# Block products of the gate/up weights in the second half's FFN, from weight sums kept in DRAM

## The chip, the core and the metric

The kernel runs on one core of one Trainium2 chip. The metric is the time of one execution on the device in microseconds (us), from runs on the chip. A core has TensorE (PE: matmuls, with PEld its weight loads), VectorE (DVE), ScalarE (ACT), GpSimd (POOL) and SyncE (SP). Each engine works through its own instructions in the order in which they stand in the built program and waits at semaphores for the others. SP and POOL issue DMA transfers. Matmuls write to PSUM, which the kernel uses in banks of 512 columns; the other tiles lie in SBUF.

## The reference, cut to what matters

One layer: a conditioned norm, two branches (a gated linear recurrence and chunked linear attention), their merge, and a feed-forward network (FFN). There are 1024 tokens of a prompt and 32 of a sample group (8 sequences of 4), D_MODEL is 1024 and D_FF 2816, all in fp32. What is changed is the first product of the FFN:

```
h2 = _rmsnorm(x, norm2_g) * (1.0 + sc2) + sh2
f1, f2 = jnp.split(h2 @ ffn_w1, 2, axis=-1)
x = (x + gt2 * ((jax.nn.silu(f1) * f2) @ ffn_w2))
```

## The kernel before

Activations lie with features on the 128 partitions and tokens on the columns. `h2` is 8 tiles of 128 features (the k tiles). The kernel works the tokens in two halves one after the other: half A has 512 prompt tokens, half B the other 512 and the 32 sample tokens, 544 columns, in two parts of 272 (p0, p1). Names end in `a` or `b` for the half.

Every fp32 operand is split in two: hi is the operand rounded to the type fp32r (a copy on ScalarE, L141), lo the rest (a subtraction on VectorE, L142). A product takes three matmuls for each k tile and part (L365 to L367 in `gemm`): hi by hi, hi weights by lo input, lo weights by hi input. `load_raw` gets a weight tile of 128 x 1024 from DRAM through SP into one of three `raw` buffers; `split_w` writes it, hi and lo, into one of three `hl` buffers, with a raised priority.

The FFN has 22 couples, one gate tile (`f1`) and one up tile (`f2`) of 128 rows of ffn_w1 each. `pair` computes a couple: the gate product into one PSUM tile, tanh and a VectorE operation for the silu, the up product into a second PSUM tile, the multiplication with it, and the split of the result `fa` for the second FFN product. In half B a PSUM tile (pool `mm`) has two banks, and there are three of them; in half A six of one bank.

`back` sets the order at the FFN: output projection, norm2, then couples 0 to 3 (EARLY) first for part p0 and then, in reverse, for part p1 (`ffn1_first`, woven into the norm by `mix`), then couples 4 to 10 for the whole half (`ffn1`), then the first half of the second FFN product (`ffn2`). Couples 11 to 21 follow in the main program at the end of the function. A scheduler that has a model of the engines puts the instructions of each engine in order; a product may be interleaved with others there.

Of the kernel before, what the change touches and what calls it, by code (L numbers as in the profile page):

```python
# [7 lines left out]
F32 = mybir.dt.float32  # L8
F32R = mybir.dt.float32r
I32 = mybir.dt.int32  # L10
AF = mybir.ActivationFunctionType
OP = mybir.AluOpType
# [3 lines left out]
P = 128  # L16
# [11 lines left out]
LEVELS = (64, 32, 16, 8, 4, 2, 1)  # L28
EPS = 1e-6
EARLY = 4  # L30
AHEAD = 70
def starts_of(w):
    return [min(i, w - P) for i in range(0, w, P)]
# [19 lines left out]
def hybrid_layer(ctx, tc, I, O):  # L53
# [17 lines left out]
    xp = ctx.enter_context(tc.tile_pool(name="xp", bufs=8))  # L71
    tp = ctx.enter_context(tc.tile_pool(name="tp", bufs=6))
    axp = ctx.enter_context(tc.tile_pool(name="axp", bufs=2, space=PSUM))

    def S(name, dt=F32):
        return sbig.tile([P, 2 * 544], dt, tag="S", name=name)
# [216 lines left out]
    def drain(g):  # L293
        for _ in g:
            pass
# [29 lines left out]
    class Half:  # L325
# [23 lines left out]
        def psv(s, ps, part):  # L349
            return s.pv(ps) if part[2] is None else ps[:, part[2], part[3]:part[3] + part[1]]  # L350

        def gemm(s, ps, hl, nk, rhs, k0=0, first=True, last=True, part=None, hk=0, split=None):
            N = s.N
            if part is None:
                pieces = split or ([(0, HP, 0, 0)] if s.hf == 0 else s.parts)
            else:
                pieces = [part]
            for kt in range(nk):
                x = rhs[k0 + kt]
                wh = hl[:, 0, (hk + kt) * P:(hk + kt + 1) * P]  # L360
                wl = hl[:, 1, (hk + kt) * P:(hk + kt + 1) * P]
                st, en = first and kt == 0, last and kt == nk - 1
                for o, w, bank, off in pieces:
                    out = ps[:, bank, off:off + w]
                    pe.matmul(out, wh, x[:, o:o + w], start=st, stop=False)  # L365
                    pe.matmul(out, wh, x[:, N + o:N + o + w], start=False, stop=False)  # L366
                    pe.matmul(out, wl, x[:, o:o + w], start=False, stop=en)  # L367
# [777 lines left out]
        def pair(s, f, part, a):  # L1145

            n = f"{s.n}{f}{part[2]}{part[0]}"
            whole = part[2] is None
            gp = None if whole else part
            ti = (lambda t: s.sv(t)) if whole else (lambda t: t)  # L1150
            o, w = part[0], part[1]
            p1 = mm("f1ps" + n)
            fr = not whole and o == 0
            s.gemm(p1, load_kept(("f1", f), I["ffn1"][2 * f], 1024, "f1" + n, fr and f == EARLY - 1), 8, s.h2, part=gp)
            yield w * 24 / 2400.0
            tg = T("ft" + n)[:, :w]
            v1 = s.psv(p1, part)
            act.activation(ti(tg), v1, AF.Tanh, scale=0.5)
            dve.scalar_tensor_tensor(ti(tg), ti(tg), 1.0, v1, op0=OP.add, op1=OP.mult)
            p2 = mm("f2ps" + n)  # L1160
            s.gemm(p2, load_kept(("f2", f), I["ffn1"][2 * f + 1], 1024, "f2" + n, fr and f >= EARLY - 2), 8, s.h2, part=gp)
            dve.tensor_mul(ti(tg), ti(tg), s.psv(p2, part))
            hi, lo = a[:, o:o + w], a[:, s.N + o:s.N + o + w]
            act.activation(hi, tg, AF.Copy)
            dve.tensor_sub(lo, tg, hi.bitcast(F32))
            yield w * 24 / 2400.0

        def ffn1_first(s, part, n):
            for f in range(n) if part[0] == 0 else range(n - 1, -1, -1):
# [44 lines left out]
        def back(s):  # L1214
# [12 lines left out]
            next(f)  # L1227
            mix(s.norm2(p1, a1), f)
            drain(f)
            drain(s.ffn1_first(p1, EARLY))  # L1230
            drain(s.ffn1(0, EARLY))
            drain(s.ffn2(0, s.whole))

        def branches(s, before):
# [49 lines left out]
    drain(dn)  # L1284
    mm_pool(2)
    B.branches(A.finish(A.whole, acc))
    drain(B.ffn1(1))
    p0, p1 = B.parts
    a0, a1 = [ACC("30b")], [ACC("31b")]
    drain(B.ffn2(1, p0, a0))  # L1290
# [32 lines left out]
def _pack(inp):  # L1323
# [30 lines left out]
    a["proj_b"] = _tiles(f["proj_b"][0])  # L1354
    a["w_out"] = _tiles(f["w_out"][0])
    w1 = _tiles(f["ffn_w1"][0])
    a["ffn1"] = c(w1.reshape(2, NF, P, D).transpose(1, 0, 2, 3).reshape(2 * NF, P, D))
    w2 = _tiles(f["ffn_w2"][0])
    a["ffn2"] = c(w2.reshape(KD, P, 2, 11 * P).transpose(0, 2, 1, 3).reshape(2 * KD, P, 11 * P))
# [39 lines left out]
```

## Time and profile before

| | before |
|---|---|
| time, median of 3 runs | 2015.49 us (2014.96 to 2020.08) |
| the profiled execution: time | 2014.85 us |
| the profiled execution: span of the trace | 2013.1 us |
| half A, couples 4 to 10 | from 661 to 736 us of the span |
| half B, early couples, second part | 1627.4 to 1651.5 us |
| half B, couples 4 to 10 | 1651.5 to 1735 us |
| half B, couples 11 to 21 | 1803 to 1935 us |

The span runs from the first to the last instruction in the trace; the time holds what lies around it too. The page gives busy time by engine, in all and in slices, the waits and the chain of work that ended last; the tables of windows give the same for a stretch of time. A row of a group has its line, engine and operation, what it writes and reads, how often it occurs, its busy time in us with the mean in ns, and the idle time just before it with what ended that. In a timeline the first two columns are start and duration in us. The trace gives a matmul of 272 columns a duration of 0.29 us while the next one starts 0.125 us after it: the pace is seen in the distance of starts.

### The profile page before, as it was taken

To read this page: it belongs to the slowest core of one execution; us is meant where nothing else is said; L and a number is where in the kernel's file an instruction comes from. 1 tells how busy PE (TensorE), PEld (TensorE's weight loads), DVE (VectorE), ACT (ScalarE), POOL (GpSimd) and SP (SyncE) were. 2 spreads that over 40 slices of the span, in tenths; PEclk is the share of its full clock that TensorE was granted. 3 is DMA by queue.
4 is the path that set the end of the run, shared out by engine and by line. 5 is a ranking of instruction groups with operands and counts; after the bars stand their busy time and mean duration, and the time that the engine had idled before them with its cause. 6 is when DMAs were issued, how large, how long until landed. Compare 5 with 4: busy or idle time off the path is not lost. (4 is left out here: it accounts for less than half of the span.)

```text
span 2013.1 us, 31675 instructions
## 1 busy us (share of the span) xinstructions
PE 1982.9 (99%) x13210; PEld 1782.5 (89%) x13210; DVE 1086.7 (54%) x1828; ACT 806.0 (40%) x1165; POOL 51.3 (3%) x122
## 2 busy tenths in 40 slices
PE   8999999999999999999999999999999999999997
PEld 5887777777899888888899999999999999999997
DVE  5648485544457433346473697863434763333356
ACT  3545475533245322233352465653323442222232
POOL 0000010000000000000000001110000000000000
PEclk9999999999999999999999999999999999999998
DMA  8325233334354323332422313223223442232243
GB/s 311 105 95 178 61 93 109 111 116 162 98 169 146 115 77 112 99 135 81 148 72 90 117 53 115 101 91 105 85 89 117 160 134 92 73 105 89 84 122 123
DMA packets 74639, 228.50 MB, mean 114 GB/s; under 512 B 8704, under 2 KB 16640, under 8 KB 74496
## 3 DMA queue, kind: packets, MB, share of 16 engines
q1 hardware_dynamic: 71536, 217.47, 33.6%
q0 software_dynamic: 2416, 8.44, 1.1%
q8 instruction: 104, 1.70, 0.4%
q10 hardware_dynamic: 544, 0.56, 0.1%
q14 instruction: 39, 0.32, 0.1%
HBM read 217.21 MB, written 9.23 MB: 112 GB/s over the span
## 5 line engine op out<-in xcount | busy, mean ns | idle before, releaser
L367 PE MATMUL f3psb<-fab,f3b_hl 128*128 128x272 f32 x352 | 101.4, 288 | 0.0
L365 PE MATMUL f3psb<-fab,f3b_hl 128*128 128x272 f32 x352 | 101.4, 288 | 0.0
L366 PE MATMUL f3psb<-fab,f3b_hl 128*128 128x272 f32 x352 | 100.9, 287 | 0.0
L141 ACT ACTIVATE f3b_hl<-f3b_raw 128x768 fp32r<-128x768 f32 (+1 forms) x45 | 35.7, 792 | 88.6 <-PE f3psb L367 57.2
L365 PE MATMUL f3psa<-faa,f3a_hl 128*128 128x512 f32 x176 | 68.7, 390 | 0.0
L367 PE MATMUL f3psa<-faa,f3a_hl 128*128 128x512 f32 x176 | 68.5, 389 | 0.0
L366 PE MATMUL f3psa<-faa,f3a_hl 128*128 128x512 f32 x176 | 68.5, 389 | 0.0
L365 PEld LDWEIGHTS f3psb<-fab,f3b_hl 128*128 128x128 f32 x352 | 66.4, 189 | 0.0
L367 PEld LDWEIGHTS f3psb<-fab,f3b_hl 128*128 128x128 f32 x352 | 66.2, 188 | 0.0
L366 PEld LDWEIGHTS f3psb<-fab,f3b_hl 128*128 128x128 f32 x352 | 66.1, 188 | 0.0
L142 DVE TENSOR_TENSOR f3b_hl<-f3b_raw,f3b_hl 128x768 fp32r<-128x768 f32 (+1 forms) x45 | 40.1, 892 | 35.5 <-ACT f3b_hl L141 35.2
L141 ACT ACTIVATE f3a_hl<-f3a_raw 128x768 fp32r<-128x768 f32 (+1 forms) x32 | 25.4, 793 | 84.2 <-PE f3psa L367 47.8
L142 DVE TENSOR_TENSOR f3a_hl<-f3a_raw,f3a_hl 128x768 fp32r<-128x768 f32 (+1 forms) x32 | 28.5, 890 | 39.0 <-ACT f3a_hl L141 38.3
L365 PE MATMUL uxpsb<-h1b,uxpsb_hl 128*128 128x256 f32 (+1 forms) x160 | 47.1, 294 | 0.1
L366 PE MATMUL uxpsb<-h1b,uxpsb_hl 128*128 128x256 f32 (+1 forms) x160 | 46.4, 290 | 0.0
L365 PE MATMUL ugpsb<-h1b,ugpsb_hl 128*128 128x272 f32 x160 | 46.3, 289 | 0.0
L367 PE MATMUL ugpsb<-h1b,ugpsb_hl 128*128 128x272 f32 x160 | 46.1, 288 | 0.0
L367 PE MATMUL uxpsb<-h1b,uxpsb_hl 128*128 128x256 f32 (+1 forms) x160 | 45.9, 287 | 0.0
L366 PE MATMUL ugpsb<-h1b,ugpsb_hl 128*128 128x272 f32 x160 | 45.8, 286 | 0.0
L367 PEld LDWEIGHTS f3psa<-faa,f3a_hl 128*128 128x128 f32 x176 | 33.0, 188 | 7.1 <-DVE f3a_hl L142 0.2
L366 PEld LDWEIGHTS f3psa<-faa,f3a_hl 128*128 128x128 f32 x176 | 33.1, 188 | 6.9
L365 PEld LDWEIGHTS f3psa<-faa,f3a_hl 128*128 128x128 f32 x176 | 33.0, 188 | 6.7
(1495 smaller groups left out, 7057.2 us busy)
## 6 DMA issues: line engine op xcount, KB each, us to landing
ada<-in_ada_w SPq DMA_DIRECT2D x48, 512.0 KB, 5.4
f3b_raw<-in_ffn SPq DMA_DIRECT2D x23, 384.0 KB, 3.1
f3b_raw<-in_ffn SPq DMA_DIRECT2D x22, 320.0 KB, 2.9
woa_raw<-in_w_out SPq DMA_DIRECT2D x13, 512.0 KB, 3.5
wob_raw<-in_w_out SPq DMA_DIRECT2D x13, 512.0 KB, 3.4
f3a_raw<-in_ffn SPq DMA_DIRECT2D x16, 384.0 KB, 3.1
uxpsa_raw<-in_w_in SPq DMA_DIRECT2D x10, 512.0 KB, 3.7
ugpsa_raw<-in_w_in SPq DMA_DIRECT2D x10, 512.0 KB, 3.6
```

The source lines that it names most:

```text
L141: act.activation(hl[:, 0, :n], raw[:, :n], AF.Copy)
L142: dve.tensor_sub(hl[:, 1, :n], raw[:, :n], hl[:, 0, :n].bitcast(F32))
L365: pe.matmul(out, wh, x[:, o:o + w], start=st, stop=False)
L366: pe.matmul(out, wh, x[:, N + o:N + o + w], start=False, stop=False)
L367: pe.matmul(out, wl, x[:, o:o + w], start=False, stop=en)
```

## The change

The couples 4 to 21 of half B take a scheme of Strassen's kind. The k tiles are taken as even (0, 2, 4, 6) and odd (1, 3, 5, 7), the output rows as gate and up, the columns as two parts of 272. Of these 2 x 2 x 2 blocks, eight products of 4 k tiles each become seven, of sums of blocks. The seven are called 11, t1, t2, 22, t3, 21 and t4 after the inputs that they use.

- Weight sums: when half A works a couple (4 to 21), `weight_sums` makes four sums of blocks of the raw gate and up weights on VectorE (512 columns each) and POOL sends them to DRAM (`wsum`, two transfers of 512 KB). The raw tiles of both weights are held until then.
- Input sums: `block_sums` makes the sums of blocks of `h2` and splits them, on VectorE and ScalarE. It is mixed into the p1 pass of the early couples. The result t3 is written over the columns of p0 in the even tiles.
- Products: `ffn1_fast` reads 7 blocks of 512 columns a couple, as pairs in a raw tile, four of them from `wsum`. 11, t2, t3 and t4 add up in one bank of PSUM tile x (`f1ps`), t1 and 22 in the other; 21 goes to tile y (`f2ps`). Between them ScalarE copies the running values out (`snap`, into `va` and `vb`), and VectorE adds the rest.
- `pair` and the packing of ffn_w1 use the k tiles in the order KORD, evens first, in both halves.

In half B the couples after the change have no `pair`; in half A and in the early couples they have.

On TensorE, at the start of couple 7 of half B (`f1psb7` is its tile x): before, the gate product runs through its k tiles, three rows for each.

```order
L365 MATMUL f1psb7None0_15133<-h2b00_14027,f1b7None0_hl_15136 128x272 [waits DVE_49,Activation_49]
L366 MATMUL f1psb7None0_15133<-h2b00_14027,f1b7None0_hl_15136 128x272
L367 MATMUL f1psb7None0_15133<-h2b00_14027,f1b7None0_hl_15136 128x272 [waits DVE_49]
L365 MATMUL f1psb7None0_15133<-h2b00_14027,f1b7None0_hl_15136 128x272
L366 MATMUL f1psb7None0_15133<-h2b00_14027,f1b7None0_hl_15136 128x272
```

After, the end of couple 6's t4 (input `t42`), the last row of couple 7's 11 (input `h2b06`) and the start of its t1 (inputs `t120`, `t121`):

```order
L1241 MATMUL f1psb6_15270<-t42_14772,fwb420_hl_15378 128x272
L1242 MATMUL f1psb6_15270<-t42_14772,fwb420_hl_15378 128x272
L1242 MATMUL f1psb7_15397<-h2b06_14299,fwb420_hl_15378 128x272
L1240 MATMUL f1psb7_15397<-t120_14738,fwb422_hl_15418 128x272 [waits Activation_49]
L1241 MATMUL f1psb7_15397<-t120_14738,fwb422_hl_15418 128x272
L1242 MATMUL f1psb7_15397<-t120_14738,fwb422_hl_15418 128x272
L1240 MATMUL f1psb7_15397<-t121_14755,fwb422_hl_15418 128x272
```

The first row of t1 waits for ScalarE right behind the last row of 11; t4 of the couple before has been put in front of that last row.

On ScalarE, the same couple after the change; `vab7` and `vbb7` are the copies out of tile x, `fwb..._hl` the splits of weights, `ftb` tanh, `fab` the hi part of a result:

```order
L1246 ACTIVATE vab7_15399<-f1psb7_15397 128x272 [waits PE_49]
L145 ACTIVATE fwb426_hl_15482<-fwb426_15479 128x1024 [waits DMAHW7_49,DMAHW6_49,Activation_49]
L1274 ACTIVATE fab6_15269<-ftb6_15274 128x544 [waits DVE_49]
L1246 ACTIVATE vbb7_15400<-f1psb7_15397 128x272 [waits PE_49]
L1246 ACTIVATE vab7_15399<-f1psb7_15397 128x272 [waits PE_49]
L145 ACTIVATE fwb428_hl_15526<-fwb428_15523 128x1024 [waits DMAHW1_49,DMAHW0_49,Activation_49]
L1246 ACTIVATE vbb7_15400<-f1psb7_15397 128x272 [waits PE_49]
```

Four copies a couple stand among the splits, each with a wait for TensorE; before, ScalarE had one operation a couple that reads each gate product, and no copy.

On VectorE, in the p1 pass of half B's early couples, from the end of couple 3's p0 part (`ftb300`) on. Before:

```order
L1162 TENSOR_TENSOR ftb300_14502<-ftb300_14502,f2psb300_14505 128x272 [waits DVE_49,PE_49]
L445 SCALAR_TENSOR_TENSOR h2b07_14140<-xn2b2727_14494,mod_98,h2b07_14140 128x272 [waits Activation_49]
L1165 TENSOR_TENSOR fab3_14455<-ftb300_14502,fab3_14455 128x272 [waits Activation_49]
L142 TENSOR_TENSOR f1b21272_hl_14597<-f1b21272_raw_14595,f1b21272_hl_14597 128x1024 [waits DMAHW7_49,Activation_49]
L1159 SCALAR_TENSOR_TENSOR ftb31272_14563<-ftb31272_14563,f1psb31272_14538 128x272 [waits Activation_49]
```

After:

```order
L1171 TENSOR_TENSOR ftb300_14666<-ftb300_14666,f2psb300_14669 128x272 [waits DVE_49,PE_49]
L1196 TENSOR_TENSOR d00_14727<-h2b00_14191 128x544
L449 SCALAR_TENSOR_TENSOR h2b07_14304<-xn2b2727_14658,mod_118,h2b07_14304 128x272 [waits Activation_49]
L1174 TENSOR_TENSOR fab3_14619<-ftb300_14666,fab3_14619 128x272 [waits Activation_49]
L1196 TENSOR_TENSOR d10_14728<-h2b01_14196 128x544
L1197 TENSOR_TENSOR ta0_14729<-d00_14727 128x272 [waits DVE_49]
L1199 TENSOR_TENSOR tb0_14730<-d10_14728,d00_14727 128x272 [waits DVE_49]
L1198 TENSOR_TENSOR ta0_14729<-d10_14728,ta0_14729 128x272 [waits DVE_49]
L146 TENSOR_TENSOR f1b21272_hl_14831<-f1b21272_raw_14829,f1b21272_hl_14831 128x1024 [waits DMAHW7_49,Activation_49]
L1200 TENSOR_TENSOR tb0_14730<-d10_14728,ta0_14729 128x272 [waits DVE_49]
```

The operation that reads `f1psb31272` (couple 3's gate product for p1) and so frees that PSUM tile came one split later; now 23 operations of the block sums stand ahead of it, of which the piece shows the first.

The diff, without some of its context:

```diff
 EARLY = 4
+KORD = (0, 2, 4, 6, 1, 3, 5, 7)
+QW = 272
...
     xp = ctx.enter_context(tc.tile_pool(name="xp", bufs=8))
     tp = ctx.enter_context(tc.tile_pool(name="tp", bufs=6))
     axp = ctx.enter_context(tc.tile_pool(name="axp", bufs=2, space=PSUM))
+    drp = ctx.enter_context(tc.tile_pool(name="drp", bufs=1, space=bass.MemoryType.DRAM))
+    wsum = {f: drp.tile([P, 2048], F32, name=f"wsum{f}") for f in range(EARLY, NF)}
     def S(name, dt=F32):
         return sbig.tile([P, 2 * 544], dt, tag="S", name=name)
...
         def psv(s, ps, part):
             return s.pv(ps) if part[2] is None else ps[:, part[2], part[3]:part[3] + part[1]]
-        def gemm(s, ps, hl, nk, rhs, k0=0, first=True, last=True, part=None, hk=0, split=None):
+        def gemm(s, ps, hl, nk, rhs, k0=0, first=True, last=True, part=None, hk=0, split=None, order=None):
             N = s.N
             if part is None:
                 pieces = split or ([(0, HP, 0, 0)] if s.hf == 0 else s.parts)
             else:
                 pieces = [part]
             for kt in range(nk):
-                x = rhs[k0 + kt]
+                x = rhs[order[kt] if order else k0 + kt]
                 wh = hl[:, 0, (hk + kt) * P:(hk + kt + 1) * P]
                 wl = hl[:, 1, (hk + kt) * P:(hk + kt + 1) * P]
                 st, en = first and kt == 0, last and kt == nk - 1
...
             o, w = part[0], part[1]
             p1 = mm("f1ps" + n)
             fr = not whole and o == 0
-            s.gemm(p1, load_kept(("f1", f), I["ffn1"][2 * f], 1024, "f1" + n, fr and f == EARLY - 1), 8, s.h2, part=gp)
+            r1 = r2 = None
+            if whole:
+                r1, r2 = load_raw(I["ffn1"][2 * f], 1024, "f1" + n), load_raw(I["ffn1"][2 * f + 1], 1024, "f2" + n)
+            s.gemm(p1, split_w(r1, 1024, "f1" + n) if whole else load_kept(("f1", f), I["ffn1"][2 * f], 1024, "f1" + n, fr and f == EARLY - 1), 8, s.h2, part=gp, order=KORD)
             yield w * 24 / 2400.0
             tg = T("ft" + n)[:, :w]
             v1 = s.psv(p1, part)
             act.activation(ti(tg), v1, AF.Tanh, scale=0.5)
             dve.scalar_tensor_tensor(ti(tg), ti(tg), 1.0, v1, op0=OP.add, op1=OP.mult)
             p2 = mm("f2ps" + n)
-            s.gemm(p2, load_kept(("f2", f), I["ffn1"][2 * f + 1], 1024, "f2" + n, fr and f >= EARLY - 2), 8, s.h2, part=gp)
+            s.gemm(p2, split_w(r2, 1024, "f2" + n) if whole else load_kept(("f2", f), I["ffn1"][2 * f + 1], 1024, "f2" + n, fr and f >= EARLY - 2), 8, s.h2, part=gp, order=KORD)
+            if whole:
+                s.weight_sums(f, r1, r2)
             dve.tensor_mul(ti(tg), ti(tg), s.psv(p2, part))
             hi, lo = a[:, o:o + w], a[:, s.N + o:s.N + o + w]
             act.activation(hi, tg, AF.Copy)
             dve.tensor_sub(lo, tg, hi.bitcast(F32))
             yield w * 24 / 2400.0
+        def weight_sums(s, f, r1, r2):
+            u, v = S(f"wu{f}"), S(f"wv{f}")
+            dve.tensor_add(u[:, 0:512], r2[:, 0:512], r2[:, 512:1024])
+            dve.tensor_sub(u[:, 512:1024], u[:, 0:512], r1[:, 0:512])
+            dve.tensor_sub(v[:, 512:1024], r1[:, 0:512], r2[:, 0:512])
+            dve.tensor_sub(v[:, 0:512], r1[:, 512:1024], u[:, 512:1024])
+            pool.dma_start(wsum[f][:, 0:1024], u[:, :1024])
+            pool.dma_start(wsum[f][:, 1024:2048], v[:, :1024])
+        def block_sums(s):
+            N, W = s.N, QW
+            s.bs = {k: [] for k in ("11", "21", "22", "t1", "t2", "t3", "t4")}
+            t4 = None
+            for i in range(4):
+                h0, h1 = s.h2[2 * i], s.h2[2 * i + 1]
+                d0, d1, ta, tb = T(f"d0{i}"), T(f"d1{i}"), T(f"ta{i}"), T(f"tb{i}")
+                for d, h in (d0, h0), (d1, h1):
+                    dve.tensor_add(d, h[:, :N].bitcast(F32), h[:, N:2 * N].bitcast(F32))
+                dve.tensor_sub(ta[:, :W], d0[:, :W], d0[:, W:])
+                dve.tensor_sub(ta[:, W:], d1[:, :W], ta[:, :W])
+                dve.tensor_sub(tb[:, :W], d1[:, :W], d0[:, :W])
+                dve.tensor_sub(tb[:, W:], d1[:, W:], ta[:, W:])
+                if i % 2 == 0:
+                    t4 = S(f"t4{i}", F32R)
+                t12 = S(f"t12{i}", F32R)
+                o4 = i % 2 * W
+                for t, o, src in (t12, 0, ta), (t4, o4, tb[:, W:]), (h0, 0, tb[:, :W]):
+                    w = 2 * W if src is ta else W
+                    act.activation(t[:, o:o + w], src, AF.Copy)
+                    dve.tensor_sub(t[:, N + o:N + o + w], src, t[:, o:o + w].bitcast(F32))
+                for k, t, o in (("11", h0, W), ("21", h1, W), ("22", h1, 0), ("t1", t12, 0), ("t2", t12, W),
+                                ("t3", h0, 0), ("t4", t4, o4)):
+                    s.bs[k].append((t, o))
+                yield 1.0
+        def ffn1_fast(s, fs):
+            N, W = s.N, QW
+            units = []
+            for f in fs:
+                w1, w2, sm = I["ffn1"][2 * f], I["ffn1"][2 * f + 1], wsum[f]
+                units += [w1[:, 0:512], sm[:, 0:512], sm[:, 512:1024], sm[:, 1024:1536], sm[:, 1536:2048], w1[:, 512:1024],
+                          w2[:, 512:1024]]
+            now = [0, None]
+            def weights():
+                u = now[0]
+                now[0] += 1
+                if u % 2 == 0:
+                    raw = wp.tile([P, 1024], F32, tag="raw", name=f"fw{s.n}{fs[0]}{u}")
+                    two = units[u:u + 2]
+                    for j, src in enumerate(two):
+                        sp.dma_start(raw[:, j * 512:(j + 1) * 512], src)
+                    now[1] = split_w(raw, 512 * len(two), f"fw{s.n}{fs[0]}{u}")
+                return now[1], u % 2 * 512
+            def product(out, key, first):
+                hl, c = weights()
+                for i, (x, o) in enumerate(s.bs[key]):
+                    wh, wl = hl[:, 0, c + i * P:c + (i + 1) * P], hl[:, 1, c + i * P:c + (i + 1) * P]
+                    xh, xl = x[:, o:o + W], x[:, N + o:N + o + W]
+                    pe.matmul(out, wh, xh, start=first and i == 0, stop=False, skip_group_check=True)
+                    pe.matmul(out, wh, xl, start=False, stop=False, skip_group_check=True)
+                    pe.matmul(out, wl, xh, start=False, stop=i == 3, skip_group_check=True)
+            def snap(dst, ps):
+                with tc.high_priority(AHEAD):
+                    act.activation(dst, ps, AF.Copy)
+            for f in fs:
+                n = f"{s.n}{f}"
+                a = S("fa" + n, F32R)
+                x, y = mm("f1ps" + n), mm("f2ps" + n)
+                pa, pb, pc = x[:, 0, :W], x[:, 1, :W], y[:, 0, :W]
+                v1, v2, tg = T("va" + n), T("vb" + n), T("ft" + n)
+                hi, lo = slice(0, W), slice(W, 2 * W)
+                product(pa, "11", True)
+                snap(v1[:, lo], pa)
+                product(pb, "t1", True)
+                snap(v2[:, lo], pb)
+                product(pa, "t2", False)
+                snap(v1[:, hi], pa)
+                product(pb, "22", False)
+                yield 6
+                product(pa, "t3", False)
+                snap(v2[:, hi], pa)
+                dve.tensor_add(v1[:, hi], v1[:, hi], pb)
+                product(pc, "21", True)
+                dve.tensor_add(v1[:, lo], v1[:, lo], pc)
+                dve.tensor_add(v2[:, hi], v2[:, hi], v2[:, lo])
+                act.activation(tg, v1, AF.Tanh, scale=0.5)
+                dve.scalar_tensor_tensor(tg, tg, 1.0, v1, op0=OP.add, op1=OP.mult)
+                dve.tensor_mul(tg[:, hi], tg[:, hi], v2[:, hi])
+                product(pa, "t4", False)
+                dve.tensor_mul(tg[:, lo], tg[:, lo], pa)
+                act.activation(a[:, :N], tg, AF.Copy)
+                dve.tensor_sub(a[:, N:2 * N], tg, a[:, :N].bitcast(F32))
+                s.act.append(a)
+                yield 4.5
         def ffn1_first(s, part, n):
             for f in range(n) if part[0] == 0 else range(n - 1, -1, -1):
...
             next(f)
             mix(s.norm2(p1, a1), f)
             drain(f)
-            drain(s.ffn1_first(p1, EARLY))
-            drain(s.ffn1(0, EARLY))
+            if s.hf:
+                b = s.block_sums()
+                mix(s.ffn1_first(p1, EARLY), b)
+                drain(b)
+                drain(s.ffn1_fast(range(EARLY, 11)))
+            else:
+                drain(s.ffn1_first(p1, EARLY))
+                drain(s.ffn1(0, EARLY))
             drain(s.ffn2(0, s.whole))
         def branches(s, before):
...
     drain(dn)
     mm_pool(2)
     B.branches(A.finish(A.whole, acc))
-    drain(B.ffn1(1))
+    B.act = []
+    drain(B.ffn1_fast(range(11, NF)))
     p0, p1 = B.parts
     a0, a1 = [ACC("30b")], [ACC("31b")]
     drain(B.ffn2(1, p0, a0))
...
     a["proj_b"] = _tiles(f["proj_b"][0])
     a["w_out"] = _tiles(f["w_out"][0])
     w1 = _tiles(f["ffn_w1"][0])
+    w1 = w1.reshape(2 * NF, P, KD, P)[:, :, list(KORD)]
     a["ffn1"] = c(w1.reshape(2, NF, P, D).transpose(1, 0, 2, 3).reshape(2 * NF, P, D))
     w2 = _tiles(f["ffn_w2"][0])
     a["ffn2"] = c(w2.reshape(KD, P, 2, 11 * P).transpose(0, 2, 1, 3).reshape(2 * KD, P, 11 * P))
```

## The prediction, made before the changed kernel was run

> **What bounds the kernel now.** I read the busy line of the page first, then the table of windows around the stage that changes, then TensorE's own waits there.
>
> ```profile
> PE 1982.9 (99%) x13210; PEld 1782.5 (89%) x13210; DVE 1086.7 (54%) x1828; ACT 806.0 (40%) x1165; POOL 51.3 (3%) x122
> ```
> ```profile
> 1600.00:1627.00 27.00, 25.74 (x197) 24.56 (x196) 24.37 (x77) 14.02 (x26) 0.00 (x0) 1.00 0.44 146
> 1627.40:1651.50 24.10, 24.10 (x196) 24.10 (x195) 15.07 (x26) 10.89 (x17) 0.00 (x0) 1.00 0.40 132
> 1655.00:1667.00 12.00, 12.00 (x98) 12.00 (x98) 4.53 (x5) 3.18 (x4) 0.00 (x0) 1.00 0.27 89
> 672.00:736.00 64.00, 64.00 (x284) 53.03 (x283) 25.01 (x30) 17.93 (x24) 0.00 (x0) 1.00 0.27 87
> ```
> ```profile
> PE f1psb L366 <- DVE h2b L445: 0.6, 1, 0.6
> PE f1psb L365 <- ACT h2b L444: 0.4, 1, 0.4
> ```
> The columns of a window are its length and the busy time of PE, PEld, DVE, ACT and POOL. TensorE is the bound: it never stops in the couples (1655 to 1667) nor in the pass over the second part of the early couples (1627.4 to 1651.5). Before that pass it waits about 1 us, for the norm. So matmuls removed are time removed, **if nothing else stops TensorE**. VectorE is the engine to watch: 4.53 of 12.0 us in the couples, but 15.07 of 24.1 in the pass, and 24.37 of 27.0 just before it, where it has no room.
>
> **Matmuls removed.** The tile answer gives a start for each couple's last copy:
>
> ```profile
> L1164 ACT ACTIVATE fab<-ftb5None x1: 645/645/645, 1676.4 to 1676.4; 128x544 fp32r<-128x544 f32 x1
> L1164 ACT ACTIVATE fab<-ftb8None x1: 645/645/645, 1712.3 to 1712.3; 128x544 fp32r<-128x544 f32 x1
> ```
> Three couples take 35.9 us, so one takes 11.97 and each of its 96 matmuls of 272 columns 0.1247 us. Seven products of 12 are 84: 18 couples lose 216 matmuls, **-26.9 us**.
>
> **Hand-overs added.** The products 11, t1, t2, 22, t3 and t4 share the PSUM tile x, and copies on ScalarE take their running values out. As the PE rows of the built order show, t1's first matmul waits for ScalarE although the copy reads the other bank: the wait is for the tile. So 11, copy, t1, copy, t2, copy, 22 are serial. One such hand-over, from a timeline:
>
> ```profile
> 1681.07 0.29 PE L367 MATMUL f1psb6None<-h2b,f1b6None_hl 128*128 128x272 f32 x1
> 1681.39 0.63 ACT L1158 ACTIVATE ftb6None<-f1psb6None 128x544 f32<-128x544 f32 x1 [4.31 <-PE f1psb6None L367]
> ...
> 1616.58 0.40 ACT L387 ACTIVATE rb2b<-rps2b 128x272 f32<-128x272 f32 x1 [0.66 <-PE rps2b L384]
> ...
> 1601.35 0.52 ACT L444 ACTIVATE h2b<-xn2b,mod 128x272 fp32r<-128x272 f32 x1
> 1601.92 0.19 PEld L365 LDWEIGHTS f1psb<-h2b,f1b_hl 128*128 128x128 f32 x1 [0.67 <-ACT h2b L444]
> 1601.93 0.39 PE L365 MATMUL f1psb<-h2b,f1b_hl 128*128 128x272 f32 x1 [0.45 <-ACT h2b L444]
> ...
> 1602.96 0.39 PE L366 MATMUL f1psb<-h2b,f1b_hl 128*128 128x272 f32 x1 [0.64 <-DVE h2b L445]
> 1603.19 0.29 PE L367 MATMUL f1psb<-h2b,f1b_hl 128*128 128x272 f32 x1
> ```
> ScalarE starts 0.32 us after the last matmul's start, copies 272 columns in 0.40, and TensorE restarts 0.06 after the end: 0.78, where the next matmul would have come after 0.125. That is 0.655 lost. After a wait a matmul shows 0.39 instead of 0.29 and the next one comes 0.23 behind, not 0.125: 0.10 more. So a hand-over costs **0.76 us less 0.125 for each matmul put in between**. The PE order puts product 21 and the next couple's 11 there. In odd couples (7, 9, ...) it puts 0 matmuls after 11, 2 after t1 and 4 after t2: 0.76 + 0.51 + 0.26. Between t3 and t4 stand a copy and an addition on VectorE, 0.76 + 0.46 = 1.22, against 8 matmuls: 0.22. Sum 1.75. In even couples it puts 2, 6 and 4: 0.51 + 0 + 0.26 = 0.77, and a weight split stands just before the copy on ScalarE, up to 0.2 more: 0.85. The mean is 1.3, times 18 **+23.4 us**. (In even couples 11 matmuls, 1.37 us, cover the 1.22.) The bounds are 0 (all covered) and 3 x 0.76 + 1.22 = 3.5 a couple (nothing covered). The order names the fill, so I stay by it. Behind the waiting matmul stands all of TensorE; a copy itself waits only for its product and for the split ahead of it on ScalarE.
>
> ScalarE and VectorE hold this pace by the rows of a weight split (1.06 and 1.22 us for 1024 columns): 3.5 splits, 4 copies, tanh and copy make 6.6 us of ScalarE a couple; splits, five operations of 272 and two of 544 make 7.9 of VectorE; a couple takes 11.8.
>
> ```profile
> L141 ACT ACTIVATE f1b_hl<-f1b_raw 128x1024 fp32r<-128x1024 f32 x7 | 7.4, 1057 | 7.4 <-PE f2psb L367 4.9 <-issue 1.6 <-PE f1psb L367 0.9
> L142 DVE TENSOR_TENSOR f1b_hl<-f1b_raw,f1b_hl 128x1024 fp32r<-128x1024 f32 x7 | 8.6, 1224 | 2.9 <-ACT f1b_hl L141 2.9
> L1092 DVE TENSOR_TENSOR gab<-gab,mbb 128x544 f32<-128x544 f32 x8 | 5.8, 719 | 0.0
> L1165 DVE TENSOR_TENSOR fab<-ftb,fab 128x272 fp32r<-128x272 f32 x8 | 3.5, 434 | 0.0
> 1300.86 5.17 DVE L176 TENSOR_TENSOR ybb<-srb,ybb 128x544 fp32r<-128x544 f32 x8
> ```
>
> **Input block sums.** They add 12 VectorE operations of 544 columns and 24 of 272. With 0.719 and 0.434 that is 19.0 us; back to back, eight of 544 took 5.17, or 0.645 each, so 0.36 for 272: 16.4. VectorE had 15.07 of 24.1 us in this pass, and t1 of couple 4 needs all of the sums. So it wants 31.5 to 34.1 us, 7.4 to 10.0 too many. In the DVE order the first sums stand ahead of the operation that frees couple 3's first PSUM tile; the weight splits and the products' own operations queue behind them too. With three PSUM tiles TensorE runs on and then stops. **+8.7 us**, the middle. It is less only if TensorE had other work there, and the order has none.
>
> **A cold restart.** These stops will be some 5 and 3 us. At the end of this kernel TensorE waited 2.2 us:
>
> ```profile
> PE rps3b L384 <- DVE rstd3b L290: 2.2, 1, 2.2
> 2002.00:2004.00 2.00, 0.00 (x0) 0.00 (x0) 1.65 (x11) 0.00 (x0) 0.00 (x0) 0.50 0.00 0
> 2004.07 1.48 PE rps3b L384 x6
> 1586.49 0.84 PE rps2b L384 x6
> ```
> The granted clock was 0.50 and six small matmuls took 1.48 instead of 0.84. After the first stop VectorE is still late, so slowness hides in the second; behind the second it counts. I take **+1.0** between 0 and 3. The Trainium skill (TensorE: Matmul & The Clock Gate, section "Part 1: The HAM clock gate") says that the clock halves after an idle window of about 3.4 us and returns after as long a busy one; the 0.50 here came sooner. By that rule 3.4 us at half speed lose 1.7, twice 3.4, and the sum would be 2026.4.
>
> **Order of the k tiles.** Early couple 0 follows the norm's tiles as they come, two VectorE operations of 0.49 each:
>
> ```profile
> L431 DVE SCALAR_TENSOR_TENSOR xn2b<-xmb,gains,rb2b 128x272 f32<-128x272 f32 x16 | 7.6, 494 | 0.0
> L445 DVE SCALAR_TENSOR_TENSOR h2b<-xn2b,mod,h2b 128x272 fp32r<-128x272 f32 x16 | 7.5, 495 | 0.2 <-ACT h2b L444 0.2
> ```
> Now tile 6 comes fourth. Before, 28 matmuls stood ahead of the first that needs a late tile, now 18: 10 x 0.125 = 1.25 us. The first half is alike (33 and 27, and the tile one step later). I take 1.3 in each, **+2.6**, between 0 and 5.
>
> **Weight sums in the first half.** Four operations of 512 columns a couple, 2.7 us by the row below, on a VectorE that works 25.01 of 64 us there (4.2 per couple of 10.85): hidden, **0**. The two DMA of 512 KB that POOL issues per couple lie beside transfers at 87 GB/s in that window, against 403 at the start of the kernel.
>
> ```profile
> L743 DVE TENSOR_TENSOR wa<-wa,ka 128x512 f32<-128x512 f32 x12 | 8.2, 687 | 0.2 <-ACT wa L732 0.2
> 8.00:10.00 2.00, 2.00 (x5) 0.91 (x4) 1.91 (x8) 1.85 (x4) 0.00 (x0) 1.00 1.00 403
> f1a_raw<-in_ffn SPq DMA_DIRECT2D x7, 512.0 KB, 4.2
> out_gla_s<-s0b POOLq DMA_DIRECT2D x8, 512.0 KB, 3.3
> ```
>
> **The sum.** The profiled execution took 2014.85 us (span 2013.1), 0.64 under the median. -26.9 + 23.4 + 8.7 + 1.0 + 2.6 = +8.8, so 2023.7, on the median's footing **2024.0**. About 0.3% (6 us) is what a measurement of this kernel can tell from no change.
>
> **Rivals.** (a) *Products run densely.* If the copies hid behind the fill, +23.4 goes: 2000.6, faster. For it: 24 matmuls of 21 and the next 11 could cover 3.0 us. Against it: the order puts them elsewhere. 0.07. (b) *Weights wait loaded.* The rows at 1601.92 show load and matmul starting together after a wait; were the load done during it, 0.10 would go at six waits in two couples, 54 x 0.10 = 5.4: 2018.6, no change. 0.13. The Trainium skill (same page, "Architectural detail") says that TensorE's queue can pull weight loads ahead of matmuls in flight, which would give that; the row at 1601.92 speaks against it. (c) *Block sums covered*, if VectorE's short operations overlap more: 2015, no change. 0.04. (d) *First-half loads become late.* Both raw tiles of a couple are now held until its sums are made, with three buffers. From the sums' end to the next use stand landing 4.2, splits 1.06 + 1.22, and the sums 2.7: 9.2 of 10.85 us. If landing takes over 5.8 with the writes beside it, each further us costs 18: at 6.8, 2042, slower. 0.06. (e) *The cold restart costs both times*: 2026.4, slower. 0.06.
>
> **How the numbers follow.** The forecast has 0.64, its own range 2019 to 2030 (block sums 7.4 to 10, tile order 0 to 5, hand-overs 0.2 a couple either way); a quarter of it lies under 2021.5. Slower: 0.48 + 0.06 + 0.06 = 0.60. Same: 0.16 + 0.13 + 0.04 = 0.33. Faster: 0.07. The range 2012.5 to 2031 leaves out (a) and (d) and a little of the tails.
>
> **What would show it.** Couples of the second half start 11.8 us apart, not 10.5; PE's waits name ScalarE's copies (vab, vbb) with 0.2 to 0.8 us each; two stops of PE on VectorE's ftb operation in the early couples' second pass, 8 to 9 us together; no new wait in the first half's couples. If couples start 10.5 apart, the hand-over price is wrong; if the pass still takes 24 us, the block sums are.

## The result, and the profile after

| | before | after |
|---|---|---|
| time, median of 4 runs | 2016.99 us (2014.96 to 2020.08) | 2032.01 us (2030.88 to 2035.48) |
| the profiled execution | 2014.85 us | 2030.88 us |

The ratio is 1.0076, with a 95% interval of 1.0057 to 1.0095: slower by some 15 us. The forecast was 2024.0, with a range up to 2031. Between the two profiled executions lie 16.0 us where 8.8 were forecast.

The busy time by engine of the page, then TensorE's waits in the second half from the norm on (engine and line that waited, what it waited for, us in all, times, longest), then its waits in the couples of the first half, where it had none before:

```profile
PE 1981.2 (98%) x12994; PEld 1764.7 (87%) x12994; DVE 1195.7 (59%) x2036; ACT 868.4 (43%) x1277; POOL 71.4 (4%) x158
```
```profile
PE f2psb L369 <- DVE ftb L1166: 6.0, 2, 5.1
PE f1psb L1240 <- ACT vab L1246: 4.4, 10, 0.5
...
PE f2psb L369 <- DVE fxwb L1113: 2.1, 1, 2.1
PE f1psb L1240 <- ACT vbb L1246: 1.9, 8, 0.2
...
PE f3psb L371 <- DVE f3b_hl L146: 0.5, 2, 0.2
```
```profile
PE f2psa20None L369 <- ACT f2a20None_hl L145: 2.7, 1, 2.7
PE f2psa20None L371 <- DVE f2a20None_hl L146: 0.5, 1, 0.5
```

216 matmuls are gone (13210 to 12994), but TensorE is busy for only 1.7 us less: matmuls at a low clock last longer (0.63 us instead of 0.39 for 512 columns in couple 20 of the first half), and a row of 272 columns lasts 0.29 us where the next one could start after 0.125, so that the first part of a short wait behind it counts as busy. The main waits are of four kinds: for VectorE while it makes block sums (`ftb`), for the copies (`vab`, `vbb`), for the norm (`fxwb`), and one that the forecast said would not be there, for the up weights of couple 20 in the first half. The table of windows shows the stages; its columns are those of the prediction, with the granted clock third from the end:

```profile
1605.90:1636.80 30.90, 28.27 (x206) 27.09 (x205) 25.64 (x80) 14.87 (x28) 0.00 (x0) 0.94 0.40 129
1636.80:1669.60 32.80, 26.70 (x194) 26.08 (x193) 30.53 (x63) 16.44 (x29) 0.00 (x0) 0.90 0.31 97
1693.20:1705.00 11.80, 11.79 (x89) 11.02 (x88) 7.65 (x11) 6.40 (x11) 0.00 (x0) 1.00 0.42 137
672.00:736.00 64.00, 64.00 (x284) 53.01 (x283) 38.37 (x54) 19.00 (x24) 6.39 (x12) 1.00 0.53 178
894.80:911.10 16.30, 13.04 (x49) 10.00 (x48) 12.29 (x18) 5.91 (x9) 2.13 (x4) 0.90 0.54 175
```

The first two rows are the early couples' first and second pass of the second half. The second pass takes 32.8 us instead of 24; VectorE is busy in 30.5 of them. In a couple (third row) VectorE has 7.65 and ScalarE 6.40 of 11.8 us, close to the 7.9 and 6.6 forecast. The fourth row holds couples of the first half at full pace in spite of the sums. The last is couple 20 there: 16.3 us instead of 10.9, with the clock at 0.90 on average.

From the starts of the stages' first matmuls in both timelines (us); after the change the second FFN product starts ahead of the last couple's t4, whose 12 matmuls (1.5 us) are counted with the couples:

| stage | before | after | difference | forecast |
|---|---|---|---|---|
| second half, couples 4 to 10 and 11 to 21 | 83.6 + 131.4 | 82.6 + 130.0 | -2.5 | -26.9 + 23.4 |
| second half, early couples, second pass | 23.9 | 32.8 | +8.9 | +8.7 + 1.0 |
| early couples in the first half | 49.6 | 50.6 | +1.0 | +1.3 |
| second half, early couples, first pass | 28.2 | 30.9 | +2.7 | +1.3 |
| first half, couple 20 | 10.9 | 16.35 | +5.5 | 0 |
| the rest | | | +0.4 | 0 |

### The profile page after: what moved, and what is told of

It is laid out like the page before. It is cut to its first block, busy times and chain, and to the rows that moved or that the text cites. A ratio compares the mean times of both kernels' runs of the same rounds, so it can differ in the third digit from the quotient of the medians.

```text
span 2029.1 us, 31859 instructions
## 1 busy us (share of the span) xinstructions
PE 1981.2 (98%) x12994; PEld 1764.7 (87%) x12994; DVE 1195.7 (59%) x2036; ACT 868.4 (43%) x1277; POOL 71.4 (4%) x158
## 5 line engine op out<-in xcount | busy, mean ns | idle before, releaser
L146 DVE TENSOR_TENSOR fwb_hl<-fwb,fwb_hl 128x1024 fp32r<-128x1024 f32 (+1 forms) x64 | 77.2, 1206 | 61.4 <-ACT fwb_hl L145 61.0
L145 ACT ACTIVATE fwb_hl<-fwb 128x1024 fp32r<-128x1024 f32 (+1 forms) x64 | 66.7, 1042 | 36.0 <-PE f1psb L1242 22.1
L1240 PE MATMUL f1psb<-t,fwb_hl 128*128 128x272 f32 x216 | 67.0, 310 | 6.4 <-ACT vab L1246 4.4
L1240 PE MATMUL f1psb<-h2b,fwb_hl 128*128 128x272 f32 x216 | 63.7, 295 | 0.0
L1241 PE MATMUL f1psb<-t,fwb_hl 128*128 128x272 f32 x216 | 62.1, 287 | 0.0
L1242 PE MATMUL f1psb<-t,fwb_hl 128*128 128x272 f32 x216 | 62.0, 287 | 0.0
L1242 PE MATMUL f1psb<-h2b,fwb_hl 128*128 128x272 f32 x216 | 62.0, 287 | 0.0
L1241 PE MATMUL f1psb<-h2b,fwb_hl 128*128 128x272 f32 x216 | 62.0, 287 | 0.0
L1240 PEld LDWEIGHTS f1psb<-t,fwb_hl 128*128 128x128 f32 x216 | 40.5, 188 | 15.1 <-ACT vab L1246 8.4
```

The costliest lines, as they stand in the source:

```text
L145: act.activation(hl[:, 0, :n], raw[:, :n], AF.Copy)
L146: dve.tensor_sub(hl[:, 1, :n], raw[:, :n], hl[:, 0, :n].bitcast(F32))
L1240: pe.matmul(out, wh, xh, start=first and i == 0, stop=False, skip_group_check=True)
L1241: pe.matmul(out, wh, xl, start=False, stop=False, skip_group_check=True)
L1242: pe.matmul(out, wl, xh, start=False, stop=i == 3, skip_group_check=True)
```

## The experiments

A run's time is a median beside runs of the kernel before on the same chip: 2017.24 us (2013.66 to 2019.68, 15 runs) for the first four, 2015.06 (2013.03 to 2017.27, 9 runs) for the last four. The changed kernel ran in a series of its own, so a run is set against it by the two ratios to the kernel before: a difference of 0.001 is 2.0 us. By the two 95% intervals such a difference is uncertain by some 4.6 us either way, so that the -4.4 of experiments 3 and 6 rest on the traces and not on the medians alone.

### 1. The weight sums alone

The edit to the kernel before, in `pair` (`sums` is true for whole couples of the first half):

```
+            if sums:
+                r1, r2 = load_raw(I["ffn1"][2 * f], 1024, "f1" + n), load_raw(I["ffn1"][2 * f + 1], 1024, "f2" + n)
...
+            if sums:
+                s.weight_sums(f, r1, r2)
```

> The kernel before plus the first half's weight sums (four VectorE operations a couple, two writes to DRAM that nothing reads, both raw tiles held until the sums are made); the second half is that of before. Theory C (collision): the sums are hidden except in couple 20, where they stand in VectorE's queue among the second half's norm sums, hold the raw tile longer, and the next up load comes late: a stop of about 3 us there, a low clock behind it, 5 to 6 us in all, about 2021. Theory H (the prediction's term): hidden everywhere, 0. Theory L (loads late throughout): 0.3 to 0.6 us in each of the 18 couples, 5 to 10 us with no single stop.

2021.86 us, ratio 1.0023 (1.0013 to 1.0032), +4.6. Couple 20 took 15.6 us instead of 10.9, and no other couple changed. TensorE's waits there:

```profile
PE f2psa20None L367 <- ACT f2a20None_hl L143: 2.0, 1, 2.0
...
PE f2psa20None L369 <- DVE f2a20None_hl L144: 0.5, 1, 0.5
```

Theory C holds, H and L fall. The timeline of the changed kernel shows how (in brackets what ended the wait before an instruction):

```profile
892.72 0.72 DVE L404 TENSOR_TENSOR acc1b<-acc1b,sq1b 128x544 f32<-128x544 f32 x1 [0.90 <-ACT sq1b L402]
893.36 0.68 DVE L1180 TENSOR_TENSOR wu<-f2a19None_raw 128x512 f32<-128x512 f32 x1
...
895.83 0.69 DVE L1182 TENSOR_TENSOR wv<-f1a19None_raw,f2a19None_raw 128x512 f32<-128x512 f32 x1
896.44 0.72 DVE L404 TENSOR_TENSOR acc1b<-acc1b,sq1b 128x544 f32<-128x544 f32 x1
896.58 0.33 SPq L136 DMA_DIRECT2D f2a20None_raw<-in_ffn  x1
...
902.00 1.06 ACT L145 ACTIVATE f2a20None_hl<-f2a20None_raw 128x1024 fp32r<-128x1024 f32 x1 [3.58 <-DMA f2a20None_raw<-in_ffn]
...
903.11 0.50 PE L369 MATMUL f2psa20None<-h2a,f2a20None_hl 128*128 128x512 f32 x1 [2.73 <-ACT f2a20None_hl L145]
```

The second half's norm sums its squares (`acc1b`) while the first half still works couples 19 to 21. Those additions wait for ScalarE's squares (`sq1b`) and so for the second half's input, and VectorE takes its instructions in order: couple 19's weight sums stand behind and between them. The raw tile is free only when the sum of L1182 ends, at 896.5, and SP then issues the load of couple 20's up weights. It lands after 5.4 us, is split, and TensorE starts the up product at 903.1. Before, the same load was issued 21 us sooner and that product started at 899.9:

```profile
875.32 0.33 SPq L132 DMA_DIRECT2D f2a20None_raw<-in_ffn  x1
```

Not all of the 21 us are the norm's. Since the raw tiles are held until the sums are made, all up weights come late after the change: the lo part of couple 18's was ready 1.2 us ahead of the first matmul that reads it, couple 19's 0.8. Couple 19's up load was issued at 881.9, and a couple takes 10.9, so 896.6 is 3.8 us behind the rhythm of the loads. That is more than the margin that was left.

### 2. The order of the k tiles alone

```
+KORD = (0, 2, 4, 6, 1, 3, 5, 7)
-                x = rhs[k0 + kt]
+                x = rhs[order[kt] if order else k0 + kt]
+    w1 = w1.reshape(2 * NF, P, KD, P)[:, :, list(KORD)]
```

> The kernel before with only the new order of the k tiles (weights packed and products run as 0,2,4,6,1,3,5,7). The prediction's term: +2.6 us, 1.3 in each half, no low clock. Theory G (gate): +3.7 us as between the two traces, 1.0 in the first half; 2.7 in the second, of which 1.3 is the longer wait on the late tiles and 1.4 the low granted clock behind it. Rival: 0, and the 2.7 us belong to the weight loads of the changed kernel.

2023.75 us, ratio 1.0032 (1.0019 to 1.0044), +6.5. In its profiled execution the early couples take 1.1 us more in the first half and the first pass of the second half 2.6, close to theory G, and the pass after it 0.35 more. The rest of the difference lies where nothing was changed: 1.8 us ahead of the early couples, and 3.0 at a low clock near 1278 us (last section). All five executions lie between 2022.2 and 2024.6, so more than the 4.1 us of these stages comes in each of them; what it is in the others, the one trace cannot say. The size on the median is not clean; the wait and the clock are. Waits, then windows around it:

```profile
PE f2psb L366 <- DVE fxwb L1110: 2.1, 1, 2.1
```
```profile
1608.00:1612.00 4.00, 2.55 (x13) 2.58 (x14) 3.50 (x10) 1.29 (x3) 0.00 (x0) 0.75 0.52 170
1612.00:1616.00 4.00, 4.00 (x29) 4.00 (x28) 1.27 (x4) 1.61 (x3) 0.00 (x0) 0.82 0.00 0
```

The same 2.1 us stand behind the norm as in the changed kernel, and the clock falls behind them. That speaks against the rival: the kernel before has neither block products nor sums.

### 3. Weight sums ahead of the norm

```
-            dve.tensor_add(u[:, 0:512], r2[:, 0:512], r2[:, 512:1024])
+            with tc.high_priority(AHEAD):
+                dve.tensor_add(u[:, 0:512], r2[:, 0:512], r2[:, 512:1024])
...
```

> The changed kernel with the weight sums put ahead of the second half's norm sums in VectorE's queue; all work stays. Theory C: the up load of couple 20 starts some 4 us sooner, the stop and the low clock behind it go, -5 to -6 us against the changed kernel, about 2025.5. Rival D (transfers): the load is late because the second half's input (four loads of 544 KB) and the two writes of sums take the DMA engines in those 15 us; then the stop stays, 0 to -2 us.

2027.73 us, ratio 1.0054 (1.0041 to 1.0066). Against the changed kernel's 1.0076 that is -4.4 us (the expected times of this series were reckoned from its profiled 2030.88). The load of couple 20's up weights:

```profile
L136 SPq DMA_DIRECT2D f2a20None_raw<-in_ffn x1: 328/328/328, 889.2 to 889.2; - x1
```

It is issued at 889.2 instead of 896.6, couple 20 takes 10.87 us, and TensorE has no wait in the first half's couples. The input loads and the writes of sums are all still there, so transfers (rival D) were not the cause. The edit moves the sums ahead in every couple, not only beside the norm: the split of couple 19's up weights was done at 881.5 instead of 889.0. So it shows that the late place of the sums in VectorE's queue was the cause; how much of it was the norm's additions, and how much the margin that was thin already, it does not separate.

### 4. Own PSUM tiles for the two running values

```
-                pa, pb, pc = x[:, 0, :W], x[:, 1, :W], y[:, 0, :W]
+                pa, pb, pc = x[:, 0, :W], y[:, 0, :W], y[:, 1, :W]
...
-                dve.tensor_add(v1[:, hi], v1[:, hi], pb)
                 product(pc, "21", True)
+                dve.tensor_add(v1[:, hi], v1[:, hi], pb)
```

> The changed kernel with pb moved out of x into the tile of pc, and product 21 issued ahead of the addition that reads pb; no copy, product or operand changes. Theory T (the hand-over price is the wait for a tile that the copy does not concern): copies lie beside the next product (1.5 us against 0.76), couples come 10.5 us apart instead of 11.8, 18 x 1.3 = -24 us against the changed kernel, about 2007. Rival E (ScalarE and VectorE, 6.6 and 7.9 us a couple by my rows, with a weight split ahead of a copy, cannot keep 10.5): couples of 11.3 or more, at most -9 us, 2022 or more.

2006.56 us (2005.87 to 2008.64), ratio 0.995 (0.9937 to 0.9962): 25.4 us under the changed kernel and faster than the kernel before. A hand-over of the changed kernel, then the starts of every second couple's last copy there, then the same copies with own tiles, and a window of two couples:

```profile
1699.84 0.40 ACT L1246 ACTIVATE vab<-f1psb 128x272 f32<-128x272 f32 x1 [0.91 <-PE f1psb L1242]
...
1700.01 0.29 PE L1242 MATMUL f2psb<-h2b,fwb_hl 128*128 128x272 f32 x1
1700.29 0.19 PEld L1240 LDWEIGHTS f1psb<-h2b,fwb_hl 128*128 128x128 f32 x1 [0.21 <-ACT vab L1246]
1700.29 0.40 PE L1240 MATMUL f1psb<-h2b,fwb_hl 128*128 128x272 f32 x1
...
1708.03 0.65 ACT L1274 ACTIVATE fab<-ftb 128x544 fp32r<-128x544 f32 x1
...
1731.72 0.65 ACT L1274 ACTIVATE fab<-ftb 128x544 fp32r<-128x544 f32 x1
```
```profile
1684.60 0.65 ACT L1274 ACTIVATE fab<-ftb 128x544 fp32r<-128x544 f32 x1
...
1705.68 0.65 ACT L1274 ACTIVATE fab<-ftb 128x544 fp32r<-128x544 f32 x1
...
1726.71 0.65 ACT L1274 ACTIVATE fab<-ftb 128x544 fp32r<-128x544 f32 x1
```
```profile
1690.00:1711.00 21.00, 21.00 (x170) 21.00 (x169) 14.95 (x22) 11.99 (x20) 0.00 (x0) 1.00 0.59 175
```

Two couples took 23.7 us and now take 21.1 or 21.0; TensorE never stops, and VectorE (7.5 a couple) and ScalarE (6.0) hold the pace, so theory E falls. The same copies are made; what is gone is the wait of a product for a copy out of the other bank of its tile. Theory T holds. (The edit also issues product 21 ahead of an addition; no run separates this small move from the tiles.)

### 5. Block sums beside two plain couples

```
-                mix(s.ffn1_first(p1, EARLY), b)
+                drain(s.ffn1_first(p1, EARLY))
+                mix(s.plain(range(EARLY, EARLY + 2)), b)
                 drain(b)
-                drain(s.ffn1_fast(range(EARLY, 11)))
+                s.last_sums()
+                drain(s.ffn1_fast(range(EARLY + 2, 11)))
```

`plain` works couples by `pair`; `last_sums` puts t3 in place out of a spare tile.

> The changed kernel with couples 4 and 5 of the second half as the twelve products of before, and the input block sums made beside them instead of in the early couples' second pass; the third sum is kept in a spare tile and put in place when couple 5 is done. Theory V (the 8.9 us of that pass are VectorE time and the low clock behind its stops): the pass takes 24 us again, two couples take 11.97 instead of 11.8, -8.5 us against the changed kernel, about 2023.5. Rival W: 17 us of sums beside 9 of the couples' own in 24 us are still too many, stops move to couple 6, -4 to -6 us, about 2027.

2024.43 us, ratio 1.0042 (1.0028 to 1.0056), -6.9 us against the changed kernel. The second pass and then the two plain couples:

```profile
1637.10:1661.30 24.20, 24.13 (x194) 23.92 (x193) 16.45 (x30) 10.89 (x17) 0.00 (x0) 1.00 0.40 131
1661.30:1685.20 23.90, 23.51 (x189) 23.32 (x189) 22.92 (x44) 11.36 (x20) 0.00 (x0) 1.00 0.36 104
```

The pass is back at 24.2 us with the clock at 1.00, and VectorE fills 22.92 of 23.9 us beside the plain couples, where TensorE stops for 0.4. Theory V holds: 8.6 us go in the pass, and the stretch from there to the second FFN product gives 1.2 of them back (113.9 us from the pass's start in the changed kernel, 106.5 here).

### 6. The natural order again

```
-                x = rhs[order[kt] if order else k0 + kt]
-                wh = hl[:, 0, (hk + kt) * P:(hk + kt + 1) * P]
+                x = rhs[k0 + kt]
+                c = order.index(kt) if order else hk + kt
+                wh = hl[:, 0, c * P:(c + 1) * P]
```

> The changed kernel with weights packed as there, but each k tile's product run in the order 0 to 7, so that the late tiles of the norm come last again. Theory G: -3.7 to -4.1 us against the changed kernel (1.1 in the first half, 1.3 of wait and 1.4 of low clock in the second), about 2028. Rival: the second half's part belongs to the weight loads or the sums on VectorE and stays, -1 us, 2031.

2026.60 us, ratio 1.0054 (1.0042 to 1.0067), -4.4 us against the changed kernel. The second half's first pass takes 28.4 us instead of 30.9; the wait for `fxwb` is 0.3 us instead of 2.1:

```profile
PE f2psb L370 <- DVE fxwb L1114: 0.3, 1, 0.3
```

So that term is the order's. All ten profiles agree: this pass took 28.2 to 28.4 us in the natural order (before, experiments 1, 6 and 8; 29.9 in experiment 7, at a low clock, last section), and 30.8 to 31.0 in the new one. That the median also fits theory G is in part luck. Of the 4.3 us between the two profiled executions 2.5 lie in this pass; 1.4 are a shorter stop at couple 20, 1.4 come from a stretch that the edit does not touch, and 1.0 go the other way.

The first half's term is not settled by this run: its early couples took 51.3 us, more than the 50.6 they were to get rid of, since the granted clock fell to 0.73 there. The ten profiles together say more. Where the clock did not fall, these couples took 48.9 to 49.6 us in the natural order (before, experiments 1 and 7) and 50.6 to 50.8 in the new one (the changed kernel, experiments 2, 3 and 4); where it fell, 50.9 and 51.3 (experiments 8 and 6) against 51.8 (5). So the order costs some 1 us or more there too. But the wait that differs is put down to a split of weights (`f1a_hl`: up to 1.2 us against 1.2 to 1.7), not to the norm's late tiles.

### 7 and 8. All four together

> The changed kernel with own tiles, weight sums first, block sums beside two plain couples and the natural order. If the four costs are separate, they add: -25.5 - 4.5 - 8.5 - 3.9, and two couples do not gain their 1.5 us, +3: 1993 against about 2017 of before, a ratio of 0.988. Rival: dense couples leave VectorE too little room for the third sums and couple 6 stops, or the loads of seven products in 10.5 us come late: 1998 or more.

1992.65 us (1990.97 to 1995.09), ratio 0.9888 (0.9874 to 0.9901): 22.4 us under the kernel before and 38 under the changed one. The forecast for it was 1993. The second pass, the plain couples and one of the dense couples:

```profile
1630.00:1653.90 23.90, 23.90 (x194) 23.90 (x193) 16.37 (x29) 10.88 (x17) 0.00 (x0) 1.00 0.40 133
1653.90:1677.80 23.90, 23.52 (x189) 23.32 (x188) 22.62 (x43) 11.40 (x20) 0.00 (x0) 1.00 0.37 105
1680.00:1690.50 10.50, 10.50 (x86) 10.50 (x86) 6.93 (x9) 5.37 (x9) 0.00 (x0) 1.00 0.52 147
```

What each experiment took away adds up: 25.4 + 4.4 + 6.9 + 4.4 = 41.1 us, less 2.6 since the two plain couples now stand in for couples of 10.5 us and no longer of 11.8, is 38.5 against the 38 measured. So within the noise the four costs were separate.

> As the run with two plain couples, with one. If VectorE's room in the pass (9 us) and in one couple (7.5 us) takes the 17 us of sums, 1.5 us less: 1991.5. If not, a stop of 1 to 4 us and perhaps a low clock: 1993 to 1997.

1998.34 us (1997.59 to 1999.64), ratio 0.9916 (0.9902 to 0.9929). That is 5.7 us more than with two plain couples, a little beyond what the second case allowed. The second pass, the plain couple, and the fast couple behind it, with the wait:

```profile
1629.10:1653.00 23.90, 23.90 (x195) 23.90 (x194) 16.37 (x29) 10.89 (x17) 0.00 (x0) 1.00 0.42 132
1653.00:1665.00 12.00, 12.00 (x99) 12.00 (x98) 11.90 (x25) 6.01 (x12) 0.00 (x0) 1.00 0.32 90
1665.00:1680.00 15.00, 11.10 (x67) 10.68 (x67) 11.12 (x20) 7.41 (x13) 0.00 (x0) 0.77 0.36 105
```
```profile
PE f1psb L1258 <- ACT vab L1264: 3.9, 1, 3.9
```

VectorE's spare time in the pass (24 less 16.4) was not used: the edit mixes the sums into the plain couple alone, so all but the first few of them stand in its queue behind the pass. One couple's room was then short, TensorE stopped for 3.9 us, and the clock fell behind the stop. The wait is put down to the copy `vab`, which ended at 1670.44, 0.06 us before TensorE went on. That copy stood in ScalarE's queue behind a copy of the block sums, which had itself waited for VectorE; VectorE's last split of t4 ended at 1670.7. So the stop comes from the sums, though the copy's name stands on it.

## Why the prediction was right or wrong, step by step

**Weight sums in the first half, 0: this step failed.** The prediction read VectorE's load from one window, couples 4 to 10 (25.01 of 64 us), called the sums hidden and put that on all 18 couples; no new wait in the first half's couples was one of its signs. In that window the sums are indeed hidden (38.37 of 64, TensorE full). At couples 19 and 20 VectorE also has the second half's norm sums, the queue is in order, and the raw tile is held by a sum that stands behind additions that wait for a DMA. The cost was 5.5 us: 3.2 of waits, and about 2.3 at a low clock and in starting again. Its size varies: in the five profiles with the sums at this place couples 20 and 21 took 2.9 to 5.5 us too long (experiment 5 least, the changed kernel most), in the three with the sums moved ahead nothing. Rival (d) had the right buffer and rightly a thin margin (9.2 of 10.85 us used), but a wrong condition: not a landing over 5.8 us (it was 5.4) in every couple, but a late release in one.

**Order of the k tiles, +2.6: too small, and right in cause for the second half alone.** It came to 1.0 in the first half and 2.7 in the second. In the second the waits named for the norm grew by 1.5 us (from 1.0 in all to 2.5), near the 1.3 of the forecast; the other 1.2 are the low clock behind them, which was not in the term. In the first half the size fits, but the wait is put down to a split of weights and not to a late tile, as the forecast had it; why the order delays that split is open.

**Matmuls and hand-overs, -3.5: right.** Couples are 11.85 us apart by the copies of couples 6 to 10, 11.8 by the stages, as forecast. The 18 couples took 212.6 us; their 18 x 84 matmuls at 0.1247 are 188.6, which leaves 24.0 for hand-overs against 23.4. Experiment 4 shows the price to be the tile's: taken away, couples come after 10.5, the 84 matmuls' own time. Rival (a), dense products, needed another layout and not another fill. Rival (b) is out: at 1700.29 load and matmul start together after the wait, as at 1601.92 before.

**Block sums, +8.7: right. Cold restart, +1.0: it did not come.** The pass grew by 8.9, of which TensorE's waits are 6.0 by the profile's rows. The clock fell behind the first stop, but there, as the prediction said itself, slowness hides in the second stop, since VectorE is late anyway; and behind the second, near 1660, where a low clock would count, it was at 1.00:

```profile
1652.00:1656.00 4.00, 4.00 (x20) 4.00 (x20) 4.00 (x8) 0.56 (x2) 0.00 (x0) 0.53 0.11 19
1660.00:1664.00 4.00, 3.40 (x27) 3.44 (x28) 3.90 (x8) 1.58 (x4) 0.00 (x0) 1.00 0.62 159
```

That the low clock cost nothing is argued from these rows; no run tried it. Experiment 5 moves the sums away and the pass is back at 24.2. Rivals (c) and (e) are out. The row that the restart's price was read from also says less than was taken from it: the clock at the end of the kernel before was 0.50 from 2002.0 on, when the wait of 2.2 us had only begun.

The sum was off by 7 us: 5.5 of the weight sums, 1.1 of the order, 1.0 of the couples, 0.8 the other way in the pass with its restart, and 0.4 outside the change. The forecast time itself has a small slip: 2014.85 + 8.8 + 0.64 is 2024.3, not 2024.0.

## What to carry to other kernels

A product scheme with fewer matmuls is worth what its running values leave of it: give every value that is copied out while others still add up a PSUM tile of its own, and look whether the next product waits for a copy that it does not need. Work put on an engine "with room" has to be weighed at every place where it will run, above all where the next stage's first operations already stand in that engine's queue, and together with the buffers that it holds. Each short stop of TensorE should be priced with the low clock that can follow.

## What the runs showed of the hardware

Short stops of TensorE can lower the granted clock, and the same stops do not do so each time. With the new order the clock fell behind the wait of 2.1 us for the norm in all five profiles, to 0.57 to 0.64 in the 4 us from the end of that wait. Shorter waits go before it: in the 4 us before its end TensorE was busy for only 1.4 to 1.5. With the natural order it was busy for 2.9 of 4 us there, and the clock stayed at 1.00 in four profiles, but fell in experiment 7, where that pass took 29.9 us instead of 28.2 to 28.4. The same window in experiments 7 and 8:

```profile
1603.00:1607.00 4.00, 3.19 (x15) 2.80 (x16) 3.62 (x10) 1.29 (x3) 0.00 (x0) 0.76 0.54 172
1603.00:1607.00 4.00, 2.81 (x19) 2.36 (x19) 3.96 (x10) 1.75 (x4) 0.00 (x0) 1.00 0.56 188
```

At two stops of about half a microsecond each, near 1270 us, that no run touched, it did not fall in the kernel before and fell to 0.50 in experiment 2, two rows of each (matmuls are also sparser there, 15 to 21 rows in 3 us where a dense window has 26):

```profile
1270.40:1273.40 3.00, 2.51 (x21) 2.42 (x22) 2.26 (x4) 2.75 (x5) 0.00 (x0) 1.00 0.83 285
1273.40:1276.40 3.00, 3.00 (x17) 2.45 (x17) 2.93 (x11) 1.43 (x2) 0.00 (x0) 1.00 0.55 172
```
```profile
1273.50:1276.50 3.00, 2.50 (x19) 2.42 (x18) 2.12 (x3) 2.60 (x5) 0.00 (x0) 0.83 0.73 229
1276.50:1279.50 3.00, 3.00 (x9) 2.42 (x9) 2.45 (x8) 0.50 (x1) 0.00 (x0) 0.50 0.50 198
```

That cost 3.0 us in experiment 2 and 1.4 in the changed kernel, from nothing that either edit did. The Trainium skill (TensorE: Matmul & The Clock Gate, section "Part 1: The HAM clock gate") says that the window in which activity is watched runs freely and that the result varies from run to run. The rows agree that it varies; that a window runs freely no run here shows. It puts the idle time that is needed at about one window of 3.4 us; here two stops of half a microsecond among sparse matmuls, or one of 2.1 us behind shorter ones, were enough. Whether this also makes up the 6 us between single runs of the kernel before was not tried.
